# Attention as 16 units in a fixed TensorE order, and the gate quarters of the decay stage moved

## The chip, the cores and the metric

One core of a Trainium2 chip. The metric is the device time of one launch in microseconds; the kernel before has a median of 1717.57 us over 3 runs (1714.52 to 1719.58).

## The reference, cut to what matters

One encoder layer over 1024 tokens of 1024 channels. The part that matters here is the two parallel mixers and their gates:

```python
a = rmsnorm(h, norm_mix)
aq, ak, av, gq, gk, gv, gr, z_f, z_b, g_att, g_gla = split_columns(a @ w_in)
y_att = windowed_gqa(rope(aq), rope(ak), av, attn_sink) @ w_branch_attn   # 8 heads, 2 kv heads, |i-j| <= 128
y_gla = gla_branch(gq, gk, gv, gr, z_f, z_b, ...) @ w_branch_gla          # decays come from z_f, z_b
h = h + (sigmoid(g_att) * y_att + sigmoid(g_gla) * y_gla) @ w_out
h = h + expert_choice_ffn(...)    # 16 experts, unchanged here
```

Attention works on 8 blocks of 128 queries; each sees its own block of keys and its two neighbours (two blocks of keys at both ends).

## The kernel before, in words

Every product in fp32 precision is three TensorE products (`mm3`): the operands are split into a high and a low part, and hi*hi, hi*lo and lo*hi are summed in PSUM. Splitting a piece of weights costs a cast on ScalarE and a subtraction on VectorE (`split`, line 131).

The stretch that the change touches runs from the start to about 419 us:

- **Prologue.** `norm_tile(t)` normalizes and turns eight tiles of tokens into `aT_h`, `aT_l`; `small_constants` and `rotary` make masks and angles on VectorE; `kv_tile` and `q_proj` follow for each tile.
- **Gates.** `gate_proj(g, q, new)` makes a quarter (256 rows) of the attention gate (g=0) or of the GLA gate (g=1): four chains of 24 products of 128x512 (96 products), each chain into a PSUM bank `mm` (two banks), then a tanh on ScalarE (line 273) and a store to `sg_d` in DRAM.
- **Decays** (line 486 on). For each of 4 heads: four pairs of products `zT`, `U` into the two `a` banks, `Abs` on ScalarE (line 496), `min` on VectorE (line 497), then `Exp` and `Ln` over the whole head on ScalarE, and 16 scans on VectorE (line 508). The tiles `lt` and `lm` have two buffers each. Quarter (0,0) stands ahead of the decays, (0,1) ahead of head 1, (0,2) ahead of head 3.
- **Attention** (`attn_block`, line 536 on). For each block of queries and each of two head pairs: scores for two heads at a time into the two `a` banks (a 128-row product, a 64-row product with the low part of k, and a mask product), `max` on VectorE (line 569), `Exp` on ScalarE (line 571), a normalization on VectorE (line 581), turned weights (`ps_tr<-ident,sm`), copies to `PT` (line 591), and products with v (`ps_b<-PT,va`, 64 columns wide). `q_tile(t)` turns the next block's queries.
- **Fill.** The table `fill` puts quarters (0,3), (1,0), (1,1) and the branch products `m1_half(0, 0)`, `m1_half(0, 1)` behind blocks 2 to 6; (1,2), `m1_half(1, 0)` and `m1_half(1, 1)` follow the last block. `m1_half` is 96 products of 128x512 with the attention output `atT`, of which each chain of 12 is multiplied by the gate on VectorE (line 615).

The order on each engine's queue is laid out at compile time by the framework's planner: it takes what is ready by its own estimates, what stands earlier in the program first. On TensorE that order can be forced: while `in_order[0]` is true, `on_pe` ties each product behind the one before. Before the change this is used only later, in the experts (line 1135). `tc.issue_after(ins)` queues what its block issues on the engine of `ins` behind `ins`, without waiting for its end. Pools are a stack: `at2` (attention) takes the room that `zu` and `lp` (decays) held, and its tiles lie in the order of their first use.

Of the kernel before, what the change touches and what calls it, by code (L numbers as in the profile page):

```python
# [67 lines left out]
def tile_hybrid_block(  # L68
# [57 lines left out]
    def turn(*args):  # L126
        return on_pe(nc.tensor.transpose(*args))  # L127
# [57 lines left out]

    def small_constants(tmpc):
# [12 lines left out]
        jp = tmpc.tile([128, 128], I32, name="jp")  # L199
        nc.gpsimd.iota(jp, pattern=[[1, 128]], base=0, channel_multiplier=-1)  # L200
        nc.vector.tensor_scalar(bmask, jp, 0.0, None, op0=ALU.is_lt)
        nc.vector.tensor_scalar(tri, jp, 0.0, None, op0=ALU.is_ge)
        nc.gpsimd.memset(ones, 1.0)
        nc.vector.tensor_scalar(nsink, sinkb, -1.0, None, op0=ALU.mult)

# [36 lines left out]

    def proj_T(ps_ap, w, half, c0, src=None, nk=KC):
# [18 lines left out]

    def gate_proj(g, q, new, w=None):

        w = w or gate_piece(g, q)
        for c in range(2):
            r0 = (q * 2 + c) * 128
            sg = new()
            for half in range(2):
                pg = bank("mm")  # L270
                proj_T(pg, w, half, c * 128)
                s1 = sg[half] if type(sg) is list else sg[:, half]
# [17 lines left out]
    identb = atA.tile([128, 128], BF16, name="identb", bufs=1)  # L290
    nc.vector.tensor_copy(identb, ident)
    amask = atA.tile([128, 2, 128], BF16, name="amask", bufs=1)
# [50 lines left out]
    with pool("wqp", behind=256) as wqp, pool("pro", bufs=2) as pro, pool("pro1") as pro1:  # L343
# [19 lines left out]
        def norm_tile(t):  # L363
# [13 lines left out]
            else:  # L377
# [3 lines left out]
                diag = pro1.tile([128, 128], F32, name="diag")  # L381
                nc.vector.tensor_scalar(diag, ident, rs[t], None, op0=ALU.mult)
            for g in range(2):
# [7 lines left out]
                sl = (slice(None), slice(g * 4, g * 4 + 4), slice(t * 128, (t + 1) * 128))  # L391
                split(aT_h[sl], aT_l[sl], pt.rearrange("p (c t) -> p c t", c=4))

        def rotary():
            invf = pro1.tile([128, 8], F32, name="invf")
            for i in range(8):
                nc.vector.memset(invf[:, i:i + 1], INV_FREQ[i])
            ang = pro1.tile([128, 8, 8], F32, name="ang")
# [136 lines left out]

    def attn_block(b):
        lo_b, hi_b = max(0, b - 1), min(NT - 1, b + 1)
        nk = hi_b - lo_b + 1
        if b % 4 == 0:
            atT[b // 4] = (ap2.tile([128, 4, 512], F32R, name="atT_h", bufs=1),  # L540
                           ap2.tile([128, 4, 512], F32R, name="atT_l", bufs=1))
        ah, al = atT[b // 4]
        qhl = qT[b]
        ks = slice(lo_b * 128, (hi_b + 1) * 128)
        n = nk * 128
        sinks = [v.rearrange("p (g c) -> p g c", g=2) for v in (sinkb, nsink)]
        for cp in range(2):

            cs = slice(2 * cp, 2 * cp + 2)
            sm = [[ap2.tile([128, 384], F32, name="sm", bufs=6) for _ in range(2)] for _ in range(2)]  # L550
            nmx = small.tile([128, 2, 2], F32, name="nmx")
            den = small.tile([128, 2, 2], F32, name="den")
            for c in range(2):
                hc = 2 * cp + c
                pss = [bank("a") for _ in range(2)]
                for g in range(2):
                    matmul(pss[g][:, 0:n], qhl[:, g, hc], kT_h[:, g, ks], start=True, stop=False)
                for g in range(2):
                    r = slice(g * 64, g * 64 + 64)
                    matmul(pss[g][:, 0:n], qhl[r, g, hc], kT_l[r, ks], start=False, stop=False)  # L560
                for g in range(2):
                    if b > 0:
                        matmul(pss[g][:, 0:128], identb, amask[:, 0], start=False, stop=b == NT - 1)
                    if b < NT - 1:
                        matmul(pss[g][:, n - 128:n], identb, amask[:, 1], start=False, stop=True)
                for g in range(2):

                    nm = nmx[:, g, c:c + 1]
                    nc.vector.tensor_reduce(nm, pss[g][:, 0:n], axis=X, op=ALU.max, negate=True)
                    nc.vector.tensor_scalar(nm, nm, 0.125, sinks[1][:, g, hc:hc + 1], op0=ALU.mult, op1=ALU.min)  # L570
                    nc.scalar.activation(sm[g][c][:, 0:n], pss[g][:, 0:n], AF.Exp, bias=nm, scale=0.125,
                                         accum_out=den[:, g, c:c + 1])
            es = small.tile([128, 2, 2], F32, name="es")
# [9 lines left out]
            po = bank("b")[:, 0:256]  # L583
            for j in range(nk):
                pt = bank("tr")
                for g in range(2):
                    for c in range(2):
                        o = (g * 2 + c) * 128
                        turn(pt[:, o:o + 128], sm[g][c][:, j * 128:(j + 1) * 128], ident)
                pT = ap2.tile([128, 512], F32, name="PT", bufs=3)  # L590
                nc.scalar.copy(pT, pt)
                for g in range(2):
                    r = slice(g * 64, g * 64 + 64)
                    matmul(po[r], va[:, lo_b + j, r], pT[:, g * 256:g * 256 + 256],
                                     start=j == 0, stop=j == nk - 1)
            qs = slice((b % 4) * 128, (b % 4) * 128 + 128)
            split(ah[:, cs, qs], al[:, cs, qs], po.rearrange("p (c t) -> p c t", c=2))

    def m1_half(half, q):

        wba_v = w_ba.rearrange("(g c d) n -> g d c n", g=2, d=64)
        hs = slice(half * 512, half * 512 + 512)
        raw = wraw.tile([128, 4, 512], F32, tag="raw", name="raw")
        for g in range(2):
            nc.sync.dma_start(raw[g * 64:(g + 1) * 64], wba_v[g][:, :, q * 512:(q + 1) * 512])
        wh, wl = [whl.tile([128, 4, 512], F32R, tag="hi", name=x) for x in ("wh", "wl")]
        split(wh, wl, raw)
        for c2 in range(2):
            sg = gp.tile([128, 2, 512], F32, tag="sgr", name="sgr", bufs=2)
            rows = slice(q * 512 + c2 * 256, q * 512 + c2 * 256 + 256)  # L610
            nc.sync.dma_start(sg, sg_d[0, rows, hs].rearrange("(c p) t -> p c t", p=128))
            for c in range(2):
                pm = bank("mm")
                proj_T(pm, (wh, wl), 0, (c2 * 2 + c) * 128, src=atT[half], nk=4)
# [12 lines left out]
    m1_half(1, 0)  # L627
    m1_half(1, 1)
    sB.close()

# [855 lines left out]
```

## Time and profile before

| | us |
|---|---|
| median of 3 runs | 1717.57 |
| profiled execution, whole | 1719.85 |
| its span | 1718.1 |
| first score product of attention starts | 211.32 |
| last product of the attention stage starts | 418.87 |
| first product of the GLA heads | 419.71 |

In the rows further below, a line of the timeline reads: start, length, engine, line of the kernel, operation, output tile <- inputs, shape, how many of them in a row; in brackets the idle time of the engine ahead of it and what ended it. Products on TensorE are pipelined and their ends are modelled, so the time of a product within a stream is read from start to start.

### The profile page before, as it was taken

How to read it: one execution, taken by the hardware profiler on the slowest of the kernel's cores; microseconds unless marked ns; L12 is line 12 of the kernel's file. 1: busy time of each engine (PE TensorE's matmuls, PEld its weight loads, DVE VectorE, ACT ScalarE, POOL GpSimd, SP SyncE). 2: the span in 40 equal slices, each digit the busy share in tenths (PEclk: the TensorE clock that was granted, in tenths of full speed). 3: DMA queues.
4: the chain of work that ended last, by engine and by line, in shares of the span. 5: the costliest groups of instructions: out<-in, count | busy, mean ns of one | idle time of the engine just before them, and what ended most of it. 6: DMA issues, size and time to landing. Idle time of an engine off the chain costs nothing. (4 is left out here: it accounts for less than half of the span.)

```text
span 1718.1 us, 23091 instructions
## 1 busy us (share of the span) xinstructions
PE 1649.0 (96%) x8795; PEld 1356.6 (79%) x8795; DVE 1175.6 (68%) x2228; ACT 903.4 (53%) x1265; POOL 155.8 (9%) x186
## 2 busy tenths in 40 slices
PE   6998999999999999999999869999999999999897
PEld 6977766667989898988887647888888887777786
DVE  7546755543474747463356878999999998888566
ACT  4235555441453535352033237777777777777632
POOL 1013300000000000000001110111111111100010
PEclk9999999999999999999999979999999999999999
DMA  6032302325112121126452589999999999992711
GB/s 233 2 106 103 130 26 62 112 85 184 50 55 69 44 80 39 49 74 226 153 197 112 189 328 383 383 395 388 392 397 390 396 387 368 377 379 90 269 50 49
DMA packets 123607, 335.06 MB, mean 195 GB/s; under 512 B 9180, under 2 KB 41988, under 8 KB 123496
## 3 DMA queue, kind: packets, MB, share of 16 engines
q1 hardware_dynamic: 106784, 277.96, 44.2%
q0 software_dynamic: 14704, 53.17, 9.1%
q10 hardware_dynamic: 2008, 2.46, 0.4%
q8 instruction: 69, 1.13, 0.3%
q14 instruction: 42, 0.34, 0.1%
HBM read 290.50 MB, written 43.06 MB: 194 GB/s over the span
## 5 line engine op out<-in xcount | busy, mean ns | idle before, releaser
L131 DVE TENSOR_TENSOR slot<-slot 128x2048 fp32r<-128x2048 f32 (+1 forms) x200 | 446.4, 2245 | 52.7 <-ACT slot L131 50.2
L131 ACT CAST slot<-slot 128x2048 fp32r<-128x2048 f32 (+1 forms) x200 | 374.8, 1879 | 103.9 <-PE ps_mm L124 56.7
L124 PE MATMUL ps_mm<-aT_h,wh 128*128 128x512 f32 x512 | 203.0, 397 | 1.2 <-ACT sgr L273 1.2
L124 PE MATMUL ps_mm<-aT_h,wl 128*128 128x512 f32 x512 | 204.1, 399 | 0.0
L124 PE MATMUL ps_mm<-aT_l,wh 128*128 128x512 f32 x512 | 203.8, 398 | 0.0
L124 PE MATMUL ps_mm<-slot,xt_h 128*128 128x512 f32 x512 | 161.6, 396 | 3.1 <-DVE slot L131 2.7
L124 PE MATMUL ps_b<-slot,xt_h 128*128 128x512 f32 x512 | 160.2, 393 | 4.0 <-DVE slot L131 4.0
L124 PE MATMUL ps_mm<-slot 128*128 128x512 f32 x576 | 142.1, 401 | 0.0
L124 PEld LDWEIGHTS ps_mm<-slot 128*128 128x128 f32 x576 | 108.1, 192 | 24.7 <-issue 1.4
L124 PEld LDWEIGHTS ps_b<-slot,xt_h 128*128 128x128 f32 x512 | 95.1, 188 | 24.8 <-DVE slot L131 5.7
L124 PEld LDWEIGHTS ps_mm<-slot,xt_h 128*128 128x128 f32 x512 | 95.7, 190 | 23.8 <-DVE slot L131 3.5
L124 PEld LDWEIGHTS ps_mm<-aT_h,wh 128*128 128x128 f32 x512 | 97.2, 190 | 18.7 <-ACT sgr L273 1.4
L124 PEld LDWEIGHTS ps_mm<-aT_h,wl 128*128 128x128 f32 x512 | 97.5, 190 | 18.3 <-issue 1.2
L124 PEld LDWEIGHTS ps_mm<-aT_l,wh 128*128 128x128 f32 x512 | 97.1, 190 | 18.3 <-issue 1.2
L131 DVE TENSOR_TENSOR wl<-raw,wh 128x2048 fp32r<-128x2048 f32 (+1 forms) x29 | 61.5, 2121 | 64.1 <-ACT wh L131 64.1
L124 PE MATMUL ps_mm<-slot,xt_l 128*128 128x512 f32 x256 | 100.4, 392 | 0.6 <-DVE xt_l L131 0.6
L131 ACT CAST wh<-raw 128x2048 fp32r<-128x2048 f32 (+1 forms) x30 | 52.1, 1735 | 92.0 <-PE ps_mm L124 87.3
L124 PE MATMUL ps_b<-slot,xt_l 128*128 128x512 f32 x256 | 99.8, 390 | 0.0
L124 PE MATMUL ps_mm<-wh,aT_l 128*128 128x256 f32 x320 | 89.4, 280 | 1.8 <-DVE aT_l L131 1.8
L124 PE MATMUL ps_mm<-wh,aT_h 128*128 128x256 f32 x320 | 90.7, 283 | 0.4 <-DVE sgr L615 0.4
L124 PE MATMUL ps_mm<-wl,aT_h 128*128 128x256 f32 x320 | 89.6, 280 | 0.0
L124 PE MATMUL ps_mm<-slot,nT_h 128*128 128x512 f32 (+1 forms) x272 | 81.8, 381 | 0.3 <-ACT nT_h L131 0.3
(381 smaller groups left out, 3311.4 us busy)
## 6 DMA issues: line engine op xcount, KB each, us to landing
slot<-in_w_exp_gate_dram SPq DMA_DIRECT2D x64, 1024.0 KB, 7.9
slot<-in_w_exp_down_dram SPq DMA_DIRECT2D x64, 1024.0 KB, 8.3
slot<-in_w_exp_up_dram SPq DMA_DIRECT2D x60, 1024.0 KB, 7.7
raw<-in_w_in_dram SPq DMA_DIRECT2D x16, 1024.0 KB, 6.6
raw<-in_w_in_dram SPq DMA_DIRECT2D x14, 512.0 KB, 5.2
sg_d<-sgr POOLq DMA_DIRECT2D x14, 512.0 KB, 3.0
xn_d<-xa POOLq DMA_DIRECT2D x8, 520.5 KB, 3.8
xt<-in_x_dram SPq DMA_DIRECT2D x8, 512.0 KB, 6.7
```

The lines of the kernel that those rows point to most:

```text
L124: return on_pe(nc.tensor.matmul(*args, **kw))
L131: return nc.scalar.copy(hi, src), eng.tensor_sub(lo, src, hi)
```

## The change

Four things change.

- **Prologue.** VectorE's copy of the positions is queued behind the scaling of the identity for tile 0; the masks, `identb`, `nsink` and the rotary angles are queued behind the last split of tile 0; the constants `invf` are written earlier.
- **Decays.** A quarter of the attention gate stands ahead of each of heads 1, 2 and 3, so that (0,3) leaves the attention stage and (0,2) stands one head earlier.
- **Attention.** `attn_block` becomes 16 units of `scores(i, c)` and `weighted(i, between)`; the scores of unit i+1 are issued ahead of the weighting of unit i. From `q_tile(0)` to the end of the stage all TensorE products are tied in program order. `sm` gets 8 buffers instead of 6.
- **Fill.** Three quarters of the GLA gate and four half branches are one generator of 160 steps (a step is one `k`: three products of 128x512). `other(n)` takes n steps: 3 between the two scores of a unit (4 from unit 8 on), one ahead of each product with v, one behind a unit. The weights of the next job are prepared half way through the current one. Attention outputs of blocks 4 to 7 are kept in free query tiles until step 96, when the first half's `atT` is done with.

```diff
 # prologue, in small_constants(tmpc, after, behind)
-        nc.vector.tensor_copy(posf, posi)
+        with tc.issue_after(after):
+            nc.vector.tensor_copy(posf, posi)
...
+        with tc.issue_after(behind):
+            nc.vector.tensor_copy(identb, ident)
+            nc.vector.tensor_scalar(bmask, jp, 0.0, None, op0=ALU.is_lt)
+            nc.vector.tensor_scalar(tri, jp, 0.0, None, op0=ALU.is_ge)
+            nc.vector.tensor_scalar(nsink, sinkb, -1.0, None, op0=ALU.mult)
...
-        norm_tile(0)
-        small_constants(pro1)
+        scaled, turned = [i.ins for i in norm_tile(0)]
+        small_constants(pro1, scaled, turned)
         norm_tile(1)
-        rotary()
+        with tc.issue_after(turned):
+            rotary()
...
 # decays
-            if h in (1, 3):
-                gate_proj(0, h // 2 + 1, new_sg)
+            if h:
+                gate_proj(0, h, new_sg)
...
 # steps: proj_T and gate_proj become generators that yield after each k
+    def steps_T(ps_ap, w, half, c0, src=None, nk=KC):
...
+            yield
...
 # attention: scores of one pair of heads
+    def scores(i, c):
...
+        pss = [bank("a") for _ in range(2)]
+        for g in range(2):
+            matmul(pss[g][:, 0:n], qhl[:, g, hc], kT_h[:, g, ks], start=True, stop=False)
+        for g in range(2):
+            r = slice(g * 64, g * 64 + 64)
+            matmul(pss[g][:, 0:n], qhl[r, g, hc], kT_l[r, ks], start=False, stop=False)
...
+    def weighted(i, between):
...
+        sm_turned(0)
+        sm_turned(1)
+        for j in range(nk):
+            between(j)
+            for g in range(2):
+                r = slice(g * 64, g * 64 + 64)
+                matmul(po[r], va[:, lo_b + j, r], pTs[j][:, g * 256:g * 256 + 256], start=j == 0, stop=j == nk - 1)
+            if j + 2 < nk:
+                sm_turned(j + 2)
...
-    fill = {2: [lambda: gate_proj(0, 3, new_sg)], 3: [lambda: gate_proj(1, 0, new_sg)], 4: [lambda: gate_proj(1, 1, new_sg)], 5: [lambda: m1_half(0, 0)], 6: [lambda: m1_half(0, 1)]}
...
+    jobs = [("g", 0), ("g", 1), ("m", 0, 0), ("m", 0, 1), ("g", 2), ("m", 1, 0), ("m", 1, 1)]
...
+    n_other, first_m1, second = [0], 64, 96
+
+    def other(n, upto=160):
+
+        for _ in range(n):
+            if n_other[0] < (upto if 0 in done else first_m1):
+                next(others, None)
+                n_other[0] += 1
+                if n_other[0] == second:
+                    at_half(1)
...
+    prepare(0)
+    at_half(0)
+    in_order[0] = True
     q_tile(0)
-    for b in range(NT):
-        if b + 1 < NT:
-            q_tile(b + 1)
-        attn_block(b)
-        for f in fill.get(b, ()):
-            f()
-    gate_proj(1, 2, new_sg)
-    m1_half(1, 0)
-    m1_half(1, 1)
+    other(1)
+    scores(0, 0)
+    other(3)
+    scores(0, 1)
+    other(2)
+    units = 2 * NT
+    for i in range(units):
+        if i + 1 < units:
+            scores(i + 1, 0)
+            other(3 if i < NT else 4)
+            scores(i + 1, 1)
+
+        def between(j):
+            other(1, 125)
+            if j == 1 and i % 2 == 0 and i + 2 < units:
+                q_tile(i // 2 + 1)
+
+        weighted(i, between)
+        if i == NT - 1:
+            done.add(0)
+        other(1, 125)
+    for _ in others:
+        pass
+    in_order[0], behind[0] = False, None
```

## Rows read from the trace of the kernel before

**Rows 1.** The page: busy time, share of the span and instructions of each engine.

```profile
PE 1649.0 (96%) x8795; PEld 1356.6 (79%) x8795; DVE 1175.6 (68%) x2228; ACT 903.4 (53%) x1265; POOL 155.8 (9%) x186
```

**Rows 2.** Windows: stretch, then PE, PEld, DVE, ACT, POOL busy, clock, DMA, GB/s.

```profile
160.00:170.00 10.00, 5.00 (x21) 3.93 (x21) 9.80 (x23) 1.87 (x4) 5.88 (x7) 0.89 0.26 107
170.00:180.00 10.00, 10.00 (x37) 8.10 (x37) 3.83 (x10) 7.21 (x6) 1.47 (x4) 0.77 0.13 52
```

**Rows 3.** Waits of PE, 120 to 420 us: total, times, longest.

```profile
PE ps_a L124 <- DVE lm L497: 6.3, 2, 3.8
PE ps_mm L124 <- DVE sgr L615: 2.2, 2, 1.8
PE ps_mm L124 <- ACT sgr L273: 1.2, 1, 1.2
```

**Rows 4.** Timeline of PE, decays: heads' zT products, a slow gate product, the first score.

```profile
145.88 0.64 PE L124 MATMUL ps_a<-zT,U 128*128 128x256 f32 x4
...
169.19 0.79 PE L124 MATMUL ps_a<-zT,U 128*128 128x256 f32 x2 [3.80 <-DVE lm L497]
169.78 0.63 PE L124 MATMUL ps_mm<-aT_h,wl 128*128 128x512 f32 x1
...
188.68 0.63 PE L124 MATMUL ps_a<-zT,U 128*128 128x256 f32 x2
...
211.32 0.36 PE L124 MATMUL ps_a<-kT_h,qT 128*128 128x256 f32 x1
```

**Rows 5.** Timeline of PE: first and last of 46 gate products in an unbroken stream.

```profile
200.13 0.39 PE L124 MATMUL ps_mm<-aT_h,wh 128*128 128x512 f32 x1
...
210.33 0.39 PE L124 MATMUL ps_mm<-aT_h,wh 128*128 128x512 f32 x1
```

**Rows 6.** Groups by line and shape, PE, from 211.3 us on: count, busy, mean, idle.

```profile
L124 PE MATMUL ps_mm<-aT_h,wl 128*128 128x512 f32 x89 | 37.5, 422 | 0.0
```

**Rows 7.** Timeline of DVE: the last scans of head 3.

```profile
203.54 1.84 DVE L508 TENSOR_TENSOR_SCAN lm<-one,lt 128x128 f32<-128x128 f32 x3
```

**Rows 8.** Timeline of ACT: the first cast of the turned queries.

```profile
208.04 1.05 ACT L530 CAST qT<-ps_tr 64x512 fp32r<-64x512 f32 x2
```

**Rows 9.** Timeline of PE, attention: scores of two heads together, then singly.

```profile
314.58 0.60 PE L124 MATMUL ps_a<-kT_h,qT 128*128 128x384 f32 x2
...
315.68 0.48 PE L124 MATMUL ps_mm<-atT_h,wh 128*128 128x512 f32 x1
...
317.86 0.34 PE L124 MATMUL ps_a<-kT_h,qT 128*128 128x384 f32 x1
...
318.61 0.42 PE L124 MATMUL ps_a<-kT_h,qT 128*128 128x384 f32 x1
...
319.42 0.48 PE L124 MATMUL ps_mm<-atT_h,wh 128*128 128x512 f32 x1
```

**Rows 10.** Timeline of PE, attention: a single gate product ahead of a product with v.

```profile
387.16 0.50 PE L124 MATMUL ps_mm<-aT_l,wh 128*128 128x512 f32 x1
387.59 0.65 PE L124 MATMUL ps_b<-PT,va 128*64 128x256 f32 x4
388.17 0.50 PE L124 MATMUL ps_mm<-aT_h,wl 128*128 128x512 f32 x1
```

**Rows 11.** Timelines of DVE and ACT: the chain behind the paired scores of rows 9.

```profile
315.80 1.02 DVE L569 TENSOR_REDUCE nmx<-ps_a 128x1 f32<-128x384 f32 x2 [7.78 <-PE ps_a L124]
...
316.99 2.28 DVE L131 TENSOR_TENSOR wl<-raw,wh 128x2048 fp32r<-128x2048 f32 x1
...
317.61 0.57 ACT L571 ACTIVATE sm<-ps_a,nmx 128x384 f32<-128x384 f32 x1
```

**Rows 12.** Timelines, prologue: a mask and the split of tile 0, and PE's wait for it.

```profile
11.27 2.28 DVE L201 TENSOR_SCALAR bmask<-jp 128x128 uint8<-128x128 int32 x1
...
16.02 0.68 DVE L131 TENSOR_TENSOR aT_l<-ps_tr,aT_h 128x512 fp32r<-128x512 f32 x1
...
16.76 0.38 PE L124 MATMUL ps_mm<-wh,aT_l 128*128 128x256 f32 x1 [1.78 <-DVE aT_l L131]
```

More of the change, by code (lines that the diff above doesn't have):

```diff
@@ L261, in gate_piece, with gate_proj, gate_steps @@
         return piece([(0, w_in[:, base + q * 256: base + (q + 1) * 256])])
-    def gate_proj(g, q, new, w=None):
+    def gate_proj(*args, **kw):
+        for _ in gate_steps(*args, **kw):
+            pass
+    def gate_steps(g, q, new, w=None, ahead=None):
         w = w or gate_piece(g, q)
         for c in range(2):
+            if c and ahead:
+                ahead()
             r0 = (q * 2 + c) * 128
@@ L270, in gate_proj @@
                 pg = bank("mm")
[L271 removed]
+                yield from steps_T(pg, w, half, c * 128)
                 s1 = sg[half] if type(sg) is list else sg[:, half]
@@ L391, in norm_tile @@
                 sl = (slice(None), slice(g * 4, g * 4 + 4), slice(t * 128, (t + 1) * 128))
-                split(aT_h[sl], aT_l[sl], pt.rearrange("p (c t) -> p c t", c=4))
+                turned = split(aT_h[sl], aT_l[sl], pt.rearrange("p (c t) -> p c t", c=4))[1]
+            return (made if t == 0 else None), turned
+        invf = pro1.tile([128, 8], F32, name="invf")
+        for i in range(8):
+            nc.vector.memset(invf[:, i:i + 1], INV_FREQ[i])
         def rotary():
-            invf = pro1.tile([128, 8], F32, name="invf")
-            for i in range(8):
-                nc.vector.memset(invf[:, i:i + 1], INV_FREQ[i])
             ang = pro1.tile([128, 8, 8], F32, name="ang")
@@ L534, in tile_hybrid_block, with around @@
     atT = {}
-    def attn_block(b):
+    S = {}
+    def around(b):
         lo_b, hi_b = max(0, b - 1), min(NT - 1, b + 1)
[L538 to L544, printed above, removed]
-        n = nk * 128
-        sinks = [v.rearrange("p (g c) -> p g c", g=2) for v in (sinkb, nsink)]
-        for cp in range(2):
-            cs = slice(2 * cp, 2 * cp + 2)
[L550 to L572, printed above, removed]
@@ new lines, in around @@
+        return lo_b, hi_b - lo_b + 1
+    sinks = [v.rearrange("p (g c) -> p g c", g=2) for v in (sinkb, nsink)]
+    def scores(i, c):
+        b, cp = i // 2, i % 2
+        lo_b, nk = around(b)
+        qhl, hc = qT[b], 2 * cp + c
+        ks = slice(lo_b * 128, (lo_b + nk) * 128)
+        n = nk * 128
+        if c == 0:
+            S[i] = ([[None] * 2 for _ in range(2)], small.tile([128, 2, 2], F32, name="nmx"),
+                    small.tile([128, 2, 2], F32, name="den"))
+        sm, nmx, den = S[i]
+        pss = [bank("a") for _ in range(2)]
[5 more added lines that the diff above has]
+        for g in range(2):
+            if b > 0:
+                matmul(pss[g][:, 0:128], identb, amask[:, 0], start=False, stop=b == NT - 1)
+            if b < NT - 1:
+                matmul(pss[g][:, n - 128:n], identb, amask[:, 1], start=False, stop=True)
+        for g in range(2):
+            sm[g][c] = ap2.tile([128, 384], F32, name="sm", bufs=8)
+            nm = nmx[:, g, c:c + 1]
+            nc.vector.tensor_reduce(nm, pss[g][:, 0:n], axis=X, op=ALU.max, negate=True)
+            nc.vector.tensor_scalar(nm, nm, 0.125, sinks[1][:, g, hc:hc + 1], op0=ALU.mult, op1=ALU.min)
+            nc.scalar.activation(sm[g][c][:, 0:n], pss[g][:, 0:n], AF.Exp, bias=nm, scale=0.125,
+                                 accum_out=den[:, g, c:c + 1])
+        if c == 1:
+            cs = slice(2 * cp, 2 * cp + 2)
@@ L582, in attn_block @@
                                             None, op0=ALU.mult)
[L583 to L595, printed above, removed]
@@ L596, in attn_block, with sm_turned @@
-            qs = slice((b % 4) * 128, (b % 4) * 128 + 128)
-            split(ah[:, cs, qs], al[:, cs, qs], po.rearrange("p (c t) -> p c t", c=2))
-    def m1_half(half, q):
+    def weighted(i, between):
+        b, cp = i // 2, i % 2
+        lo_b, nk = around(b)
+        sm = S.pop(i)[0]
+        po = bank("b")[:, 0:256]
+        pTs = {}
+        def sm_turned(j):
+            pt = bank("tr")
+            for g in range(2):
+                for c in range(2):
+                    o = (g * 2 + c) * 128
+                    turn(pt[:, o:o + 128], sm[g][c][:, j * 128:(j + 1) * 128], ident)
+            pTs[j] = ap2.tile([128, 512], F32, name="PT", bufs=3)
+            nc.scalar.copy(pTs[j], pt)
+        sm_turned(0)
+        sm_turned(1)
+        for j in range(nk):
+            between(j)
+            for g in range(2):
+                r = slice(g * 64, g * 64 + 64)
+                matmul(po[r], va[:, lo_b + j, r], pTs[j][:, g * 256:g * 256 + 256], start=j == 0, stop=j == nk - 1)
+            if j + 2 < nk:
+                sm_turned(j + 2)
+        cs = slice(2 * cp, 2 * cp + 2)
+        if b // 4 in atT:
+            at_split(b, cs, po.rearrange("p (c t) -> p c t", c=2))
+        else:
+            if cp == 0:
+                whole[b] = qtp.tile([128, 512], F32, name="qt")
+            kept[b, cp] = whole[b][:, cp * 256:cp * 256 + 256]
+            nc.scalar.copy(kept[b, cp], po)
@@ new lines, in tile_hybrid_block, with at_split, at_half, m1_piece @@
+    kept, whole = {}, {}
+    def at_split(b, cs, src):
+        ah, al = atT[b // 4]
+        qs = slice((b % 4) * 128, (b % 4) * 128 + 128)
+        split(ah[:, cs, qs], al[:, cs, qs], src)
+    def at_half(half):
+        atT[half] = (ap2.tile([128, 4, 512], F32R, name="atT_h", bufs=1),
+                     ap2.tile([128, 4, 512], F32R, name="atT_l", bufs=1))
+        for (b, cp), v in kept.items():
+            at_split(b, slice(2 * cp, 2 * cp + 2), v.rearrange("p (c t) -> p c t", c=2))
+    def m1_piece(q):
@@ L607, in m1_half, with m1_gate @@
         split(wh, wl, raw)
-        for c2 in range(2):
-            sg = gp.tile([128, 2, 512], F32, tag="sgr", name="sgr", bufs=2)
+        return wh, wl
+    m1_sg, m1_at = [], [0]
+    def m1_gate():
+        n = m1_at[0]
+        if n < 8:
+            half, r0 = n // 4, n % 4 * 256
+            hs = slice(half * 512, half * 512 + 512)
+            if n % 3:
+                sg = gp.tile([128, 2, 512], F32, tag="sgr", name="sgr", bufs=2)
+            else:
+                sg = ap2.tile([128, 2, 512], F32, name="sgm", bufs=1)
+            nc.sync.dma_start(sg, sg_d[0, r0:r0 + 256, hs].rearrange("(c p) t -> p c t", p=128))
+            m1_sg.append(sg)
+            m1_at[0] += 1
@@ L610, in m1_half, with m1_steps @@
+    def m1_steps(half, q, w, ahead=None):
+        hs = slice(half * 512, half * 512 + 512)
+        for c2 in range(2):
+            if c2 and ahead:
+                ahead()
+            if m1_at[0] != 4:
+                m1_gate()
+            sg = m1_sg.pop(0)
             rows = slice(q * 512 + c2 * 256, q * 512 + c2 * 256 + 256)
-            nc.sync.dma_start(sg, sg_d[0, rows, hs].rearrange("(c p) t -> p c t", p=128))
             for c in range(2):
                 pm = bank("mm")
-                proj_T(pm, (wh, wl), 0, (c2 * 2 + c) * 128, src=atT[half], nk=4)
+                yield from steps_T(pm, w, 0, (c2 * 2 + c) * 128, src=atT[half], nk=4)
@@ L626, in tile_hybrid_block, with prepare, all_steps @@
-    gate_proj(1, 2, new_sg)
-    m1_half(1, 0)
-    m1_half(1, 1)
+    jobs = [("g", 0), ("g", 1), ("m", 0, 0), ("m", 0, 1), ("g", 2), ("m", 1, 0), ("m", 1, 1)]
+    ws = {}
+    def prepare(n):
+        if n < len(jobs):
+            kind, *at = jobs[n]
+            ws[n] = gate_piece(1, at[0]) if kind == "g" else m1_piece(at[1])
+            if n in (2, 5):
+                m1_gate()
+    def all_steps():
+        for n, (kind, *at) in enumerate(jobs):
+            ahead = partial(prepare, n + 1)
+            yield from gate_steps(1, at[0], new_sg, ws[n], ahead) if kind == "g" else m1_steps(*at, ws[n], ahead)
```

15 lines of the change are left out of this document (7 added, 8 removed).

## The prediction

> **What bounds the kernel now.** I read the page's busy times first: TensorE is busy 96% of the span [rows 1], so only its idle time, its slow clock and what it loses between products of different shapes can be won. The windows of 10 us show where it idles in the stretch touched: 5.00 of 10 us at 160 to 170, and there and in the next window the granted clock falls to 0.89 and 0.77 [rows 2]. From 211 us to the end of the attention stage its windows stand at or near 10.00. The waits name the causes: 6.3 us for the minimum of the decays, 2.2 us for the gate tiles of the branch products, 1.2 us for a tanh [rows 3]. The timeline then shows the order: head 1's products zT start as quarter (0,1) has ended, at 145.88; the last ones of head 2 stop the queue for 3.80 us, and the gate product behind them takes 0.63 us, at the 1.2 GHz level of the clock [rows 4]. An unbroken stream of gate products costs 10.20 / 45 = 0.227 us each, at the 2.4 GHz level [rows 5].
>
> The decisive reading: quarters (0,1) to (1,2) are 576 products. From 211.3 us on 3 x 89 = 267 of them are left [rows 6], so 309 have run by the first score: all 288 of (0,1) to (0,3) and 21 of (1,0). The planner already fills the decays with quarter (0,3), and has a piece of (1,0) in hand when attention is late.
>
> **The change part by part.**
>
> *Decays.* The holes are 3.8 + 2.5 (the rest of the 6.3) + 1.2 us [rows 3], and the slow clock costs up to (0.11 + 0.23) x 10 = 3.4 us more in these two windows [rows 2]. The new order gives each quarter precedence over the products of the head that follows it. Head 1 shows what that means: it began only when quarter (0,1) was through [rows 4], though nothing of its own held it. So (0,2) runs from 146 us with less disturbance: 96 x 0.227 = 21.8 us plus head 1's own and a tanh wait end it at about 170. The weights of (0,3) need VectorE, which has room in 170 to 180 (3.83 of 10 busy [rows 2]); with a 2.3 us split I place their start at 174.5 and the end of (0,3) at 196.5. Only then do the last products of head 3 follow. Today the last of them start at 188.68 [rows 4] and the head's last scans end at 203.54 + 1.84 = 205.38 [rows 7]: a chain of 16.7 us through Abs, Exp, Ln and 16 scans. In the new order: 196.7 + 16.7 = 213.4.
>
> *What attention waits for.* `at2` lies in the room of the decays, and its first tiles are now `atT`; by the sizes in the code the first `qT` falls on the second buffer of `lt`, which is head 3's. So the first score needs head 3's end. From the cast of `qT` to the first score it was 211.32 - 208.04 = 3.3 us [rows 4, 8]. First score: 213.4 + 3.3 = 216.7; if head 3 ends as today, 208.7. These are the two bounds. In front of that score the tied order holds four transpositions and one step, three products; TensorE has nothing else, while today it takes 21 products of (1,0). I take 216.7, because the row nearest to the case, head 1 behind quarter (0,1), shows strict precedence. The idle stretch is then near 19 us, and its end at the low clock costs some 2 us as behind the 3.80 us stop [rows 4]; 1.5 us of that counts, since first units wait anyway.
>
> *Attention on TensorE.* Today from 211.32 to 419.1 it is 207.8 us: 267 gate products at 0.227 = 60.5, 192 branch products at 0.23 (nine took 2.18 us in rows 9 with the entry from another shape) = 44.2, waits 1.8, and 101.3 for the 16 units. Two scores issued together cost 315.68 - 314.58 = 1.10 us; two issued singly 319.42 - 317.86 = 1.56 [rows 9]. The new text always pairs them: 24 pairs with three blocks save 0.46 each, 8 with two about 0.3, together 13 us (nearly all are single now). Against it, each of the 44 products with v now stands between gate products. The last gate product ahead of one takes 0.43 instead of 0.23 us [rows 10]; 44 x 0.20 = 8.8 us if none were paid today; some are, I take 5.5. Sum: 101.3 - 13 + 5.5 = 93.8 (88 to 97).
>
> The Trainium skill (TensorEngine Tiling (Array Packing), Key Properties) says that tiles of the array work in parallel and that a change of tiling mode drains the array. The paired rows agree with the first, the 0.43 us with the second; by the second alone, with no parallel gain, the units would cost about 107 us and the kernel some 13 us more than I forecast, which the 1.10 us speaks against.
>
> *Waits in the tied order.* Between the scores of a unit stand three steps: 317.86 - 315.68 = 2.18 us [rows 9]. The banks come free behind two maxima, two small operations and two Exp: the second Exp ends at 317.61 + 0.57 = 318.2 [rows 11], the second product needs its bank at about 318.1. So even on free engines 0.1 us is missing in each unit: floor 1.6 us. If a weight split of 2.28 us gets in front, as it does right behind these maxima at 316.99 [rows 11], the next maxima wait for it and TensorE with everything tied behind: 7 splits x 2.3 = 16 us at worst. The other queues: `q_tile` casts and subtractions, and copies of kept outputs, add short operations. From unit 8 four steps (2.9 us) cover it. I take 6, since a split meets the tight window less than half the time. The 1.8 us wait for gate tiles is gone with their earlier load.
>
> *Sum for the stretch.* 216.7 + 285 x 0.227 (64.7) + 44.2 + 93.8 + 6 + 1.5 = 426.9, against 419.1: +7.8 us.
>
> *Prologue.* The low part of tile 0 is ready only at 16.02 + 0.68; a 2.28 us mask from 11.27 on and small operations stand in front, and TensorE waits 1.78 us [rows 12]. Moving them behind saves up to 1.8 us there; they then stand ahead of tile 1's normalization on a VectorE with little idle time, which may take it back. I take -1.3 (-1.8 to +0.5). `sm` buffers, `invf` and the moved issues on SP and GpSimd cost nothing: TensorE's stream hides them, and where it has run dry, in front of the first score, they are not what it waits for.
>
> Total: +6.5 us on a span of 1718.1. The profiled execution (1719.85 with what lies around it) is 2.3 us over the median; I put the difference on the median: 1717.57 + 6.5 = 1724.1.
>
> **The rivals.**
>
> *Head 3 slips in early (faster).* If the planner finds TensorE idle in its own estimate while (0,3) waits for its weights or a tanh, it puts head 3's products there. Head 3 then ends near 205.4 and the first score starts at 208.7. For it: the one tanh wait of 1.2 us [rows 3] is such a place. Against it: only two banks, so the third and fourth pair must wait for VectorE once more. With 4 us of waits, since the clock and the start are undisturbed: 208.7 + 64.7 + 44.2 + 93.8 + 4 = 415.4, -3.7, with the prologue -5; with the lower cost of the units (91) -8: I put 1711. It decides at a last pair near 191 us, where the sum comes to no change.
>
> *The tied order stalls at every split.* 16 instead of 6 us of waits, and VectorE's short operations on top: 1734. For it: 2.18 us against a chain of 2.5. Against it: VectorE and ScalarE are about half busy in this stage.
>
> *Half of each.* Head 3 slips in for its first pairs and ends near 209: about 1718. The change then does nothing that can be told; the move of the quarter, which the planner had made already, is paid for and won back by the pairs.
>
> **How the numbers follow.** A measurement of this kernel tells about 0.3%, 5 us. Forecast 0.42 (1718 to 1730; 0.27 beyond 0.3%, 0.15 within), early head 3 0.35 (1706 to 1716; 0.25 faster, 0.10 within), stalls 0.15 (1730 to 1737, slower), half 0.08 (within, with 0.02 faster). Faster 0.27, same 0.31, slower 0.42. The range 1707 to 1732 leaves out the top of the stalls and the bottom of the first rival. The likeliest case alone has 1718 to 1730.
>
> **What would show it.** Right: products zT of head 3 behind the last product of (0,3) near 196 us, one idle stretch of TensorE of 15 us or more in front of the first score, paired scores at 1.1 us each with waits for the maxima or Exp of a few tenths behind them, and splits in front of the longer ones. Wrong: no stretch over 8 us ahead of the first score, or the unit cost away from 88 to 97 us. If the waits in the units are over 12 us or under 2, that term is mis-sized.

## The result and the profile after

The changed kernel takes 1727.55 us (median of 5 runs, 1726.19 to 1731.03) beside 1716.21 us for the kernel before (1714.52 to 1719.58). The ratio is 1.0063, with a 95% interval from 1.0048 to 1.0077: about 11 us slower. The forecast was 1724.1 us and slower by 6.5. The profiled execution has a span of 1729.3 us, 11.2 over that of before.

The page of after, its busy times and two lines of its 40 slices (a slice is 43 us):

```profile
PE 1640.8 (95%) x8795; PEld 1347.5 (78%) x8795; DVE 1174.2 (68%) x2228; ACT 904.5 (52%) x1269; POOL 155.9 (9%) x186
...
PE   7999499999999999999999959999999999999897
...
PEclk9999799999999999999999979999999999999999
```

TensorE has the same 8795 products as before [rows 1], and its time is 8 us shorter. The fifth slice shows what went wrong: busy 4 tenths, clock 7. The windows of that place, and one further on, read as in [rows 2]:

```profile
190.00:200.00 10.00, 1.87 (x9) 0.99 (x7) 4.78 (x5) 7.89 (x9) 1.70 (x4) 0.80 0.73 213
200.00:210.00 10.00, 0.00 (x0) 0.00 (x0) 9.05 (x22) 2.20 (x2) 4.11 (x5) 0.50 0.32 102
210.00:220.00 10.00, 6.23 (x17) 4.48 (x17) 3.83 (x9) 2.29 (x7) 2.72 (x4) 0.50 0.14 55
320.00:330.00 10.00, 8.67 (x38) 5.62 (x37) 5.17 (x13) 3.07 (x9) 0.53 (x1) 0.83 0.77 210
```

TensorE does nothing at all from 200 to 210 us, while VectorE is busy 9 of 10. There and in the window behind it the granted clock is 0.50, the 1.2 GHz level. The waits of TensorE from 210 us to the end of the attention stage (the list of [rows 3], later stretch):

```profile
PE ps_a L124 <- DVE qT L548: 23.4, 7, 17.9
PE ps_mm L124 <- DVE sgr L693: 1.6, 1, 1.6
PE ps_b L124 <- ACT PT L620: 1.4, 1, 1.4
PE ps_a L124 <- ACT sm L590: 0.4, 1, 0.4
```

The timeline of TensorE gives the place, with the same tiles as [rows 4]:

```profile
189.10 0.64 PE L124 MATMUL ps_a<-zT,U 128*128 128x256 f32 x4
...
194.02 1.10 PE L124 MATMUL ps_a<-zT,U 128*128 128x256 f32 x4 [3.15 <-DVE lm L514]
212.98 0.55 PE L124 MATMUL ps_a<-kT_h,qT 128*128 128x256 f32 x1 [17.86 <-DVE qT L548]
```

The row ahead of 189.10 is the last product of quarter (0,3): strict precedence, as head 1 had shown. Then comes VectorE, last scans and first query tile (compare [rows 7]):

```profile
209.33 1.84 DVE L525 TENSOR_TENSOR_SCAN lm<-one,lt 128x128 f32<-128x128 f32 x3
...
212.15 0.68 DVE L548 TENSOR_TENSOR qT<-ps_tr,qT 64x512 fp32r<-64x512 f32 x1 [0.75 <-ACT qT L547]
```

Between the two stands ScalarE:

```profile
211.43 0.21 ACT L531 ACTIVATE em<-mid 128x16 f32<-128x16 f32 x1 [9.21 <-DVE mid L528]
211.55 0.56 ACT L547 CAST qT<-ps_tr 64x512 fp32r<-64x512 f32 x1
```

The cast for the first query tile follows `em`, the last operation of head 3, which waits for the values `mid` from the last scans. So there are two possible reasons why the cast comes no sooner: its place in ScalarE's queue, and the room of `lt`, which the prediction named. No run separates them; by both, the first score needs the end of head 3.

The account of the profiled execution: the first product of quarter (0,1) starts 2.75 us earlier (119.70 for 122.45); from there to the first score it takes 4.4 us more (93.3 for 88.9); from the first score to the last branch product 11.2 us more (219.0 for 207.8); behind that 1.7 us less. The sum is the 11.2 us of the span.

### The profile page after: what moved, and what is told of

It is laid out like the page before. It is cut to its first block, busy times and chain, and to the rows that moved or that the text cites. A ratio compares the mean times of both kernels' runs of the same rounds, so it can differ in the third digit from the quotient of the medians.

```text
span 1729.3 us, 23072 instructions
## 1 busy us (share of the span) xinstructions
PE 1640.8 (95%) x8795; PEld 1347.5 (78%) x8795; DVE 1174.2 (68%) x2228; ACT 904.5 (52%) x1269; POOL 155.9 (9%) x186
```

## The experiments

Each kernel was timed in five rounds against the kernel before on the same chip; that median lay between 1716.0 and 1717.9. "Units" below are the 16 units of attention; their cost is the time from one unit's last product with v to the next one's, less 0.227 us for each gate product and 0.23 for each branch product in between.

### The prologue alone

Before, with only the hunks on `small_constants`, `invf`, `identb` and `rotary` of the diff.

> The kernel before with the prologue part of the change alone (small operations behind the low part of tile 0). In the trace of after the key and value products of tile 0 start 2.8 us earlier than before (the 1.78 us wait is gone) and the first product of quarter (0,1) starts at 119.70 instead of 122.45. Theory A (the prologue's gain is kept to the end): 1716.2 - 2.7 = 1713.5 us, ratio 0.998. Theory B (the small operations are paid for again further down, or the attention stage starts at a time set elsewhere): 1716 us, ratio 1.000.

Measured: 1716.97 us, ratio 1.000 (0.9989 to 1.0012). Theory B. The profiled execution shows where 2 us could go. Its last branch product is 2.0 us ahead of before (416.88 for 418.87). The next product, of the value projection behind the stage, waits for a gate tile, and a window behind it has a low clock:

```profile
420.90 0.55 PE L124 MATMUL ps_mm<-wh,aT_h 128*128 128x256 f32 x1 [3.62 <-DVE sgr L620]
```

```profile
420.00:430.00 10.00, 9.10 (x57) 9.13 (x58) 3.77 (x5) 0.59 (x1) 0.72 (x1) 0.69 0.61 210
```

In before this wait was 0.44 us, part of the 2.2 us in [rows 3], and the clock 1.00. VectorE waited for the load of that tile, 7.68 us against 4.49: the load did not come earlier with the work. So a gain of 2.7 us at 120 us was worth nothing at the end. That the load takes all of it in every run is argued from one execution, which at 1722.21 us was the longest of twelve.

### The decays alone

Before, with the three quarters each ahead of a head and (0,3) gone from `fill`; attention untied.

> The kernel before with the new places of the gate quarters alone: (0,1), (0,2), (0,3) each ahead of heads 1, 2, 3 of the decays, the attention text and its untied order as before. Head 3 then ends some 10 us later than before, as in after (scans ending near 211 + 2.7). Theory A (late head 3 costs only where TensorE has nothing else to do; here it may take some 90 products of (1,0) and (1,1), 20 us, while it waits): no idle stretch over 5 us ahead of the first score, 1716 to 1720 us. Theory B (the new order of the quarters is itself the loss, whatever the order of attention): a hole of 10 us or more, 1726 us or above.

Measured: 1722.13 us, ratio 1.0029 (1.0016 to 1.0042): 5 us slower. No idle stretch of TensorE is left ahead of the first score at 215.20, for 99 products of (1,0) and (1,1) fill it; half of theory A held, its time did not. What was used up there was missing later: two neighbouring units in the middle of attention, with no step left in either, cost 9.2 and 13.6 us, where before none but one cost over 9; the clock was low there too (0.83, 0.75 and 0.90 in the three windows from 270 to 300 us).

Yet the attention stage as a whole did not lose by it: its last branch product starts at 415.61, 3.3 us ahead of before. The time goes behind it, as in the run with the prologue alone, in a wait for a gate tile and a low clock:

```profile
418.88 0.55 PE L124 MATMUL ps_mm<-wh,aT_h 128*128 128x256 f32 x1 [2.88 <-DVE sgr L615]
```

```profile
420.00:430.00 10.00, 10.00 (x69) 10.00 (x68) 2.86 (x7) 1.81 (x4) 0.34 (x1) 0.75 0.61 212
```

The profiled executions of this run and of before differ by 1.1 us (spans of 1719.2 and 1718.1), the medians by 4.6; where the rest of the loss lies the traces do not show.

### The old decays in the changed text

```diff
-            if h:
-                gate_proj(0, h, new_sg)
+            if h in (1, 3):
+                gate_proj(0, h // 2 + 1, new_sg)
...
+    gate_proj(0, 3, new_sg)
     prepare(0)
```

> After with the decays' gate quarters as before ((0,1) ahead of head 1, (0,2) ahead of head 3), and (0,3) placed behind head 3, ahead of the tied stretch, so that it may fill it. Theory A: the last products of head 3 run near 188.7 - 2.7 = 186 us, its chain of 16.7 us ends near 203, first score near 206.5 instead of 213.0; TensorE still has only 288 gate products up to there, so a hole of about 6 us stays: 1727.5 - 6.5 = 1721 us (1718 to 1724). Theory B (the hole has another cause, such as the room in which qT lies, and moves along with nothing won): 1726 us or more.

Measured: 1723.85 us, ratio 1.0037 (1.0023 to 1.0051), 6.3 us over before. The last products of head 3 start at 186.5, the first score at 209.17 behind a hole of 4.2 us:

```profile
209.17 0.36 PE L124 MATMUL ps_a<-kT_h,qT 128*128 128x256 f32 x1 [4.22 <-DVE qT L548]
```

Theory A near the upper end of its range: the 6.3 us of waits for the minimum, which after had brought to 3.2, are back. In size the two halves of the change add up: +5.0 for the decays, +6.3 for the rest with the old decays, against about +10.8 for both. Their mechanisms do not: alone, the new decays leave no hole, and the long one appears only where late decays and tie stand together.

### Untied

```diff
-    in_order[0] = True
     q_tile(0)
     other(1)
```

> After without the tied order of TensorE in the attention stage: same text, same order of emission, but the instructions may be placed as engines come free. Theory A (the loss is the empty stretch ahead of the first score, which takes both the late head 3 and the tie): the 17.9 us wait for qT and its low clock (1.9 us) go, some 100 gate products stand there, and the units lose 2 to 6 us of their pairing: 1727.5 - 20 + 4 = 1711 us (1707 to 1715). Theory B (the tied units cost as much by themselves: waits for banks, entry costs of the products with v): the hole goes and the units get cheaper as well, below 1705 us. Theory C (the pairs are what pays, untied they are lost): 1718 us or more.

Measured: **1706.31 us, ratio 0.9933 (0.9917 to 0.9949)**: 21 us under after and 11 under before. TensorE's waits from 100 to 440 us are

```profile
PE ps_mm L124 <- DVE sgr L693: 1.6, 1, 1.6
PE ps_tr L127 <- DVE sm L602: 1.0, 1, 1.0
PE ps_a L124 <- DVE qT L548: 0.8, 1, 0.8
PE ps_a L124 <- POOL zT L473: 0.3, 1, 0.3
```

Head 3 is as late as in after (first score 213.93), but 101 gate products of (1,0) and (1,1) run behind (0,3) instead of three. It ended a little under theory A's range. The units got dearer, not cheaper (112.1 us in all against 110.1), so B's reason is out. Costs by unit, in brackets the steps in between, worked out from the starts of TensorE's rows (unit 0 from the first score on; units 14 and 15, which end the stage, are the same in both):

```
unit        0        1       2      3      4      5      6       7       8      9      10     11     12     13
after    11.4(10) 6.5(6)  6.7(7) 6.9(7) 6.7(7) 6.5(7)  6.7(7)  6.3(7) 6.3(8) 9.0(8) 6.3(8) 7.4(8) 7.8(8) 6.4(8)
untied    7.7(11) 4.6(4)  7.9(3) 7.9(3) 7.2(4) 7.5(1) 11.0(1) 10.3(1) 7.2(4) 6.8(5) 6.3(8) 6.4(8) 5.9(8) 6.3(7)
```

With seven or eight steps most tied units cost 6.3 to 7 us; unit 0 stands behind the hole, and units 9, 11 and 12 have the waits listed for after. Untied with one step left, units 6 and 7 (276 to 300 us) cost 11.0 and 10.3, some 6 us together above units 2 to 5. The windows there show what most of it is:

```profile
280.00:290.00 10.00, 9.46 (x40) 5.21 (x40) 6.03 (x14) 6.63 (x17) 0.53 (x1) 0.66 0.63 174
290.00:300.00 10.00, 9.20 (x41) 5.20 (x41) 5.51 (x15) 3.39 (x10) 0.00 (x0) 0.83 0.19 37
```

The low clock costs (0.34 + 0.17) x 10 = 5.1 us, although TensorE is busy over 9 of 10 and its waits are 1.0 and 0.8 us; before it fell the engine ran turns, scores and products with v, with few gate products. That is the price of filling the hole; it is well under what the hole cost.

### The next queries turned earlier

```diff
+        if i % 2 == 0 and i + 2 < units:
+            q_tile(i // 2 + 1)
         if i + 1 < units:
             scores(i + 1, 0)
...
-            if j == 1 and i % 2 == 0 and i + 2 < units:
-                q_tile(i // 2 + 1)
```

> After with one edit: the next block's q is turned ahead of the first scores of an even unit instead of behind its second step with v, so its cast and subtraction have some 4 us more before the scores that read them. In after, six waits for qT stand between the units (23.4 - 17.9 = 5.5 us) and the longest of them drops the granted clock a second time (1.7 us). Theory A (these waits are prices of the tied order, and moving the turn removes them): 5.5 to 7 us less than after, 1727.5 - 6 = 1721.5 us. Theory B (the chain of VectorE's operations sets the pace of the units, another wait takes their place): 0 to 2 us less, 1726 us or more. The stretch ahead of the first score stays: 17.9 us.

Measured: 1732.09 us, ratio 1.0095 (1.0080 to 1.0110), some 5 us slower than after: both theories were wrong, B in size only. The waits for qT in the units fall to 0.7 us, but those for Exp grow to 4.9 and for PT to 3.4. VectorE, then TensorE:

```profile
244.58 1.02 DVE L588 TENSOR_REDUCE nmx<-ps_a 128x1 f32<-128x384 f32 x2
245.63 0.69 DVE L548 TENSOR_TENSOR qT<-ps_tr,qT 64x512 fp32r<-64x512 f32 x1
246.36 0.34 DVE L589 TENSOR_SCALAR nmx<-nmx,nsink 128x1 f32<-128x1 f32 x2
```

```profile
247.39 1.00 PE L124 MATMUL ps_a<-kT_h,qT 128*128 128x384 f32 x2 [1.00 <-ACT sm L590]
```

The subtraction for qT now stands between the maxima and the small operation on which Exp waits, and Exp frees the bank of the next scores. The Trainium skill (Perfetto Trace Analysis, Tensor Engine Instruction (MATMUL, LD_WEIGHTS)) says that VectorE, ScalarE and GpSimd work strictly in the order of their queues; these three rows agree.

### The heads spaced by 20 steps

```diff
+        quarters = (s for q in (1, 2, 3) for s in gate_steps(0, q, new_sg))
         for h in range(4):
-            if h:
-                gate_proj(0, h, new_sg)
...
+            if h < 3:
+                for _ in range(20):
+                    next(quarters)
...
+    for _ in quarters:
+        pass
     prepare(0)
```

> After with the decays' heads spaced by 20 steps of the gate quarters (60 products, 13.6 us) instead of a whole quarter, and the last 36 steps of (0,3) behind head 3; the tied order of attention as in after. Head 3's last products should then run near 175 us, its chain of 16.7 us end near 192, and TensorE has gate products until about 199, so that the first score follows them with no hole. Theory A (the hole is head 3's chain being late in an order that allows nothing else): the 17.9 us wait, its low clock (1.9 us) and the 3.2 us wait for the minimum go, 1727.5 - 21 = 1706.5 us (1703 to 1710). Theory B (the wait for qT has another cause than the place of head 3): a wait of over 5 us for qT ahead of the first score stays, 1718 us or more.

Measured: 1718.44 us, ratio 1.0015 (1.0006 to 1.0025): 8 us less than after, not 21. The wait for qT ahead of the first score is gone, and unit 0 costs 8.2 instead of 11.4 us. But the first score comes at 206.4, not at 199: the idle time has moved into the decays.

```profile
PE ps_a L124 <- DVE lm L513: 9.5, 3, 3.8
PE ps_a L124 <- DVE qT L550: 4.7, 5, 1.3
```

The rows of head 2, TensorE and what VectorE had ahead of it:

```profile
155.53 0.64 PE L124 MATMUL ps_a<-zT,U 128*128 128x256 f32 x4
...
166.10 0.50 PE L124 MATMUL ps_a<-zT,U 128*128 128x256 f32 x2 [3.84 <-DVE lm L513]
```

```profile
163.62 1.84 DVE L524 TENSOR_TENSOR_SCAN lm<-one,lt 128x128 f32<-128x128 f32 x3
165.38 0.66 DVE L513 TENSOR_SCALAR lm<-ps_a 128x512 f32<-128x512 f32 x1
```

A head takes 19.7 us from its first product (123.05) to its last scan (142.7). A head that comes sooner finds its minima behind the scans of the one before, and the two banks `ps_a` stay taken. Theory A was right on the cause of the hole, wrong on what is won by moving it.

### Spaced: without the tie, and with the other edits

The same spacing untied, and the same spacing tied with the early turn and a fourth step between the scores of units 0 to 7.

> The spaced heads without the tied order. It asks what the tie itself costs or gains once no hole needs filling. Tied units cost 6.3 to 6.9 us each beside their steps where seven or eight steps are at hand; in the untied text that filled the hole the units without steps cost 10 to 11 us. Theory A (the tie is worth its pairs, about 0.4 us per unit, against the waits it brings, 9 us): within 4 us of the tied one, 1702 to 1710 us. Theory B (the tie's waits are the larger): 1698 us or less.

> The spaced heads, the early turn of q, and in units 0 to 7 four steps between the scores of a unit instead of three (the fourth is the one that stood at the unit's end). Theory A: the two parts add up, and the bank waits behind Exp, 0.35 to 0.45 us in each of eight units, go too: 1706.5 - 6 - 3 = 1697.5 us (1694 to 1702). Theory B (with the first unit moved to a filled stretch the units meet weight splits elsewhere, and waits of the same size come back): 1703 us or more.

Measured: untied 1715.19 us (0.9987, 0.9977 to 0.9996), 3.3 us less than tied: theory A in the difference, though 5 us over its range, since the tied run itself was not at 1706.5. With the other edits 1721.44 us (1.0030, 1.0018 to 1.0042), 3 us more: theory B, by the mechanism of the early turn (waits for Exp 5.7 us, for PT 3.4). So with no hole ahead of the first score the tie still costs some 3 us, and its waits in the units are not mended by moving one instruction ahead.

### The minima ahead of the scans

`front(h)` has the products, Abs, minimum, Exp and Ln of a head, `back(h)` its subtractions and scans:

```diff
+        made = front(0)
+        for h in range(4):
+            for _ in range(20 if h < 3 else 0):
+                next(quarters)
+            then = front(h + 1) if h < 3 else None
+            back(h, *made)
+            made = then
...
+    q_tile(0)
+    for _ in quarters:
+        pass
```

> After with each head's decays in two halves: the products zT, Abs and minimum of head h+1 come ahead of the subtractions and scans of head h, with 20 steps of the gate quarters between heads, the rest of the quarters behind head 3, and q of block 0 turned ahead of that rest; attention tied as in after. In the spaced run the minima stood behind the scans of the head before on VectorE and TensorE waited 9.5 us for them, and the first score came at 206.4. Theory A (TensorE's idle time ahead of the first score is VectorE's in-order scans, wherever they stand; ahead of them the minima free the banks): waits for the minimum under 4 us, no wait for qT there, first score near 199, and the units as in the spaced run (105 us): 7 us less than that run, 1711 us (1708 to 1714). Theory B (the planner's order on VectorE is off from what happens, and the waits come back elsewhere): 1716 us or more.

> The same without the tied order in attention. In the spaced pair the tie cost 3.3 us (1718.4 against 1715.2). Theory A (costs of tie and decays add): 1711 - 3.3 = 1707.5 us (1704 to 1711), about the untied run that filled its hole with (1,0) (1706.3), in which units 6 and 7 had one step each and cost 11.0 and 10.3 us. Theory B (with no hole left, untied units keep all their steps and cost 6.3 to 7 us each, and the start is 7 us earlier than in the spaced untied run): below 1704 us.

Measured: tied 1716.67 us (1.000, 0.999 to 1.001), untied 1711.32 us (0.9973, 0.9962 to 0.9984). The first score comes at 203.7 and 203.6. Heads 1 and 2 show why only half was won. The minima of head 1 stood between scans of head 0 and no wait is left there; those of head 2 stood behind all scans of head 1 and a weight split (VectorE, then TensorE, tied run):

```profile
154.12 1.84 DVE L528 TENSOR_TENSOR_SCAN lm<-one,lt 128x128 f32<-128x128 f32 x3
155.89 2.26 DVE L131 TENSOR_TENSOR wl<-raw,wh 128x2048 fp32r<-128x2048 f32 x1
158.07 1.28 DVE L514 TENSOR_SCALAR lm<-ps_a 128x512 f32<-128x512 f32 x2
```

```profile
158.80 0.80 PE L124 MATMUL ps_a<-zT,U 128*128 128x256 f32 x2 [5.50 <-DVE lm L514]
```

For the tied run this is theory B. The untied one is 5.4 us under it, just over the range of its theory A, and the condition of its theory B, no idle time left, was not met.

### The minima forced ahead, and a wider spacing

In the first, 16 steps between heads and `back(h)` held behind the last minimum of `front(h + 1)` (`with tc.issue_after(...)`), untied. In the second, whole heads with 26 steps between them, untied.

> The front and back halves again, untied, with 16 steps between heads and the subtractions and scans of head h held behind the last minimum of head h+1 on VectorE. In the two runs before this, 5.5 us of the 8.1 us that were left fell on head 2, whose minima stood on VectorE behind 16 scans and a weight split. Theory A (the place of the minima on VectorE is all of it): waits for the minimum under 2 us, first score near 198, 1711.3 - 7 = 1704 us (1700 to 1707). Theory B (the scans then run late, and head 3's end or the weights take the place of the minima): first score after 202, 1708 us or more.

> The untied text with whole heads (no halves) spaced by 26 steps, some 20 us with the heads' own products, instead of 20 steps (three waits for the minimum, 10.0 us) or a whole quarter (no such wait, but the first score at 213.9 and units 6 and 7 without steps). A head takes 19.7 us from its first product to its last scan. Theory A (a spacing just above that length pays neither price): waits for the minimum under 2.5 us, first score near 205, some 30 products of (1,0) ahead of it, units 2 to 7 at 7 to 8 us each: 1705 us (1702 to 1708), level with the best so far (1706.3) or a little under it. Theory B (weight splits and the stores of the scanned decays still meet the next head's minima): waits of 5 us or more, 1711 us or more.

Measured: 1723.63 us (1.0040, 1.0027 to 1.0054) and 1721.00 us (1.0021, 1.0010 to 1.0031): the times of theory B in both. TensorE waited 11.9 us for minima in the first (8.6 for head 2) and 6.4 in the second. The second's theory B had named the stores of the scanned decays for the minima; that they also hold up Exp of attention was not thought of. VectorE and ScalarE of the first, ScalarE and TensorE of the second:

```profile
157.06 1.29 DVE L514 TENSOR_SCALAR lm<-ps_a 128x512 f32<-128x512 f32 x2 [6.95 <-DMA b_d<-lm]
```

```profile
214.66 0.47 ACT L602 ACTIVATE sm<-ps_a,nmx 128x256 f32<-128x256 f32 x1 [5.40 <-DMA b_d<-lm]
```

```profile
216.83 0.47 ACT L592 ACTIVATE sm<-ps_a,nmx 128x256 f32<-128x256 f32 x1 [6.11 <-DMA b_d<-lm]
```

```profile
217.45 0.58 PE L124 MATMUL ps_a<-kT_h,qT 128*128 128x256 f32 x1 [4.87 <-ACT sm L592]
```

`lm` has two buffers, and a head's buffer is free only when its scanned decays have been stored. Two heads on, the minima wait for that store; and `sm` of attention lies in the room of `lm`, so Exp waits for head 3's stores. An early first score is not enough to meet this: in the runs with front and back halves it came at 203.6, and no such wait is listed. Here the last store took 9.5 us from issue to landing in the first run and 8.5 in the second (median 2.3 in both), and landed only when Exp had long been due. During that wait the clock fell (0.50 from 213 to 215 us in the first). A run with a third buffer for `lm` was not made. The best of all kernels run is the untied one with the changed decays.

## Why the prediction was right, and where it was off

The time lay in the range and the side was right; the measured loss is 11 where 6.5 was forecast. The range of 25 us held three of the four cases nearly whole, so that the time lies in it says little; that the stretch ahead of the first score looks as it was described says more. The terms of the difference, worked out below: first score 2.4 us early, units 0.4 dearer, waits 6.3 and low clock 2.1 us more than taken, and 1.7 us less behind the stage: 4.7 us, as 11.2 less 6.5.

*Decays: right in mechanism, early by some us.* Strict precedence, the hole ahead of the first score (17.9 where near 19 was said) and its low clock came as told. Quarter (0,2) ended at 166.2, not 170, the weights of (0,3) were in time, and (0,3) ended at 189.1, not 196.5. Most of that went again: a weight split of 2.29 us got ahead of head 3's minima (the 3.15 us wait), so its last products were issued at 194 to 195, against 196.7. That this took back most of the early end is luck. The step from cast to score was 1.4 us, not 3.3 (cast at 211.55, score at 212.98): the 3.3 us read from before held a weight split, which stood on VectorE ahead of the subtraction for qT and had no counterpart in after.

```profile
208.17 2.29 DVE L131 TENSOR_TENSOR wl<-raw,wh 128x2048 fp32r<-128x2048 f32 x1 [2.59 <-ACT wh L131]
210.49 2.02 DVE L531 TENSOR_TENSOR qT<-ps_tr,qT 64x512 fp32r<-64x512 f32 x3
```

With the prologue in the sum, the first score was due at 215.4 and came at 212.98: 2.4 us to the good.

*Attention on TensorE: right.* The units were put at 93.8 us. Between first score and last branch product 219.0 us passed; less 285 gate products (64.7) and 192 branch products (44.2) that leaves 110.1 for units, waits and clock. The listed waits are 5.5 + 1.6 + 1.4 + 0.4 = 8.9, the low clock some 3.6 (nine gate products behind the hole took 3.9 us instead of 2.0, and the window at 320 has 0.83), so 97.6 stay. In this there are waits that the list doesn't show: two paired scores take 1.03 us as the first of a unit and some 1.47 as the second, in the first eight units,

```profile
242.94 0.51 PE L124 MATMUL ps_a<-kT_h,qT 128*128 128x384 f32 x2
...
243.97 0.48 PE L124 MATMUL ps_mm<-aT_h,wh 128*128 128x512 f32 x1
...
246.12 0.92 PE L124 MATMUL ps_a<-kT_h,qT 128*128 128x384 f32 x2
...
247.59 0.61 PE L127 MATMUL ps_tr<-ident,sm 128*128 128x128 f32 x4
```

about 8 x 0.43 = 3.4 us. That leaves 94.2. The Trainium skill (TensorEngine Tiling (Array Packing), Key Properties) has a drain for each change of mode beside parallel tiles; the 107 us that its drain alone would have made are not seen, with 1.03 us for a pair against 1.10 in [rows 9].

*Waits in the tied order: the term that was mis-sized.* 6 us were taken; 8.9 listed and 3.4 hidden make 12.3. The small bank wait behind three steps was 0.43, not 0.1 us in a unit. Of the rest 5.5 us are waits for qT, whose two casts and two subtractions follow each other across two engines; the prediction called them "short operations". The longest of them (ScalarE, VectorE, TensorE):

```profile
322.46 0.37 ACT L639 COPY qt<-ps_b 128x256 f32<-128x256 f32 x1 [1.49 <-PE ps_b L124]
322.90 0.58 ACT L547 CAST qT<-ps_tr 64x512 fp32r<-64x512 f32 x1
```

```profile
324.08 0.69 DVE L548 TENSOR_TENSOR qT<-ps_tr,qT 64x512 fp32r<-64x512 f32 x1
```

```profile
324.82 0.44 PE L124 MATMUL ps_a<-kT_h,qT 128*128 128x384 f32 x1 [1.33 <-DVE qT L548]
```

The second cast stands on ScalarE behind the copy of the unit's output, and that copy had waited 1.49 us for the last product with v; the waits at 351.1 and 376.7 have the same order. So it is not a weight split right in front that makes them. And the 1.8 us wait for gate tiles, which was said to be gone, is there at 1.6 us: SyncE issued the load of that tile only at 413.5 us, and VectorE stood 5.79 us for it. The low clock was sized at 1.5 us and cost 3.6, for a second spell followed the wait at 324.8. The wait alone does not explain it: one of the same length at 351.1 left the clock at 1.00.

*Prologue: the start right and more, the worth wrong.* 2.75 us were won at the first gate product, more than the 1.3; alone it was worth nothing at the end.

*The rivals.* Head 3 did not slip in early. "Half of each" was not seen either. The stalls came in part: 12.3 us of waits, where 6 were taken and this rival had 16, and the longest by another cause than splits. The cover that the prediction didn't weigh is the one that the runs found largest: the same text untied fills the hole with the gate products of later quarters and wins 21 us.

## What to carry to other kernels

A fixed order is paid where an engine runs dry: ahead of each long wait on another engine, ask which independent work the order still allows to run, and leave the order open there. Work that is pulled forward as filling is missing later, so price the stage from which it was taken as well, its clock included. When idle time moves with each edit instead of shrinking, look for the in-order queue of the other engine, and behind that for the buffers and stores that it waits for.

## What the runs showed of the hardware

The stores of the scanned decays, 256 KB each, take 2.3 us from issue to landing as a median in the run with the minima forced ahead, and 9.5 us at most; the buffer's next writer stood for 6.95 us behind one that was issued at 151.3, while the share of busy DMA was 1.05 and 1.06 in the two windows of 2 us from 152 on (a weight load had been issued at 150.1). Behind the longest, issued at 205.1, that share was 0.97 to 1.04 from 207 to 215. The Trainium skill (DMA: Bandwidth & Descriptors, Anatomy of one DMA — SWDGE (gpsimd) path) fits such a transfer by 2.0 us plus its bytes over 436,000 a microsecond; an estimate by it is 2.6 us. The median is near it; the longest one, beside weight loads, is over three times that.
